# The opening of an encoder block: idle products first, block norms and V's weights in another order, gate forms summed on VectorE

## The chip, the cores and the metric

The kernel runs on one core of a Trainium2 chip. A core has a matrix engine (PE in the profile, with its weight loads as PEld), VectorE (DVE), ScalarE (ACT), GpSimd (POOL) and SyncE (SP), which issues the DMA transfers here. Each engine works through its own instructions in the order in which the program issued them, and waits where an instruction needs something that is not there yet. The metric is the device time of one execution in microseconds (us); the times below are medians of several executions.

## The reference, cut to what matters

The kernel computes one layer of an encoder on 1024 tokens of 1024 channels, in float32:

```python
u = rms_norm(x, norm1_g)
q, k, v, cb, cc, ch, ga, gb = split(u @ w_in)      # 512 x 6, then 1024 x 2 columns
q, k = rms_norm per head (8 heads of 64)
y_a = neighbourhood_attention(q, k, v, rpb) @ w_attn_branch
y_b = (cb * conv3(cc * ch)) @ w_conv_branch
x = x + (sigmoid(ga) * y_a + sigmoid(gb) * y_b) @ w_o
x = x + relu(rms_norm(x) @ w_mlp_in)**2 @ w_mlp_out
```

The change lies in the first step, `u`, in the product for `v`, and in the preparation of `ga` and `gb`.

## The kernel before, in words

**Numbers in two halves.** Every float32 matrix is scaled by powers of two and written as two float16 matrices, a high part and a residual: ScalarE rounds (line 290 for weights, 420 for activations, 482 for forms), and a second engine subtracts the rounded value from the scaled one (lines 278 or 276, 422, 484). One product is three passes of matmuls: high by high, high by residual, residual by high. A unit of 24 matmuls does one block of 128 tokens with one group of columns over 1024 channels.

**Block norms.** x comes in eight blocks of 128 tokens. For each, the generator `norm` (line 414) squares on ScalarE with a row sum (417), then runs a chain of small VectorE operations with a square root on ScalarE in it (390 to 399), then the high part on ScalarE (420) and the residual on VectorE (422): eight steps, and `ln_step(b, n)` issues the next n of block b. Blocks 0 to 2 are transposed on PE (`ln_trans`, 424: eight transposes for each half, copied out by ScalarE and VectorE), blocks 3 to 7 by a DMA that SyncE issues (`ln_turn`, 436).

**Weights.** A `Chunk` is a group of columns: V in two chunks of 256 columns (two loads of 512 KB each), Q and K of 512 (four loads each). `prep` finds the scale (row sums on VectorE or ScalarE; a product with a tile of ones, line 179, adds over partitions; a few integer operations make a power of two of it; line 253 makes it a scale for every row) and splits the weights, load by load. Loads share five buffers, so that each later load is issued on SyncE when an earlier one has been split (line 281). For V, the second load of each chunk is scaled and subtracted on GpSimd (276, 287); all else is subtracted on VectorE (278). `tick(n)` issues the next n steps of such preparations.

**Units.** `v_unit(b, j, steps, ticks)` multiplies block b by chunk j of V (by both chunks where j is None: blocks 3 to 7), counts one more in `units`, issues the copy of the unit before it out of PSUM (508, 509), and then lets `step` and `tick` issue other work. `apart(mark, n)` makes a generator stand still until `units` has reached mark + n, so it fixes where in the order an instruction is issued, not when it runs. Q's eight units and K's eight follow, with per-head norms of what they give (`qk_vec`, 574: out of PSUM by ScalarE at 577, squared at 578, reduced at 581), and K's weights are squared while Q's units run (line 241) and split in the last of them.

**Forms for the gates.** `sforms` (467) makes four sums or differences of half rows of block n and block n + 4 for each n of 0 to 3, for a product of the gates with seven instead of eight sub-products much later: ScalarE scales the rows of the two blocks (474), GpSimd does the four sums (480), ScalarE rounds (482), VectorE subtracts (484), and `sform_store` (487) stores 1 MB to DRAM through SyncE, one unit later. The float32 sums have one buffer, the rounded forms two: the third form waits until the first has been stored. `SFORM` (465) holds the unit count at which each begins. The rows of x that it reads lie where Q's result goes later, so all four must be stored before the fourth unit of Q has ended (`formed`).

**Order around the change.** Lines 514 to 561 write it out by hand: V's first chunk and blocks 0 and 1, then V's second chunk with blocks 2 and 3, then eleven rounds p with one V unit each (from p = 1) and the steps of blocks 3 to 7, one block in two rounds at first. Q's weights are pushed at p = 3; their ones product is issued after p = 7 and their splitting follows in rounds 9 and 10.

Of the kernel before, what the change touches and what calls it, by code (L numbers as in the profile page):

```python
# [52 lines left out]
def encoder_block(ctx: ExitStack, tc: tile.TileContext, x, weights, cols, gqk, rel, masks, out):  # L53
# [79 lines left out]
    def tick(n=1):  # L133

        for _ in range(n):
            i = 0
            while i < len(bg):
                r = advance(bg[i])
                if not r:
                    bg.pop(i)  # L140
                elif r == WAIT and side[0]:
                    i += 1
                else:
                    break
# [5 lines left out]
    def flush():  # L150
        forced[0] = True
        while bg:
            tick()
            step()
        forced[0] = False
# [4 lines left out]
    def apart(mark, n=3, of=units):  # L160
        while of[0] < mark + n and not forced[0]:
            yield WAIT
# [7 lines left out]
        forced[0] = False  # L170
    ones, turn = base.tile([128, 132], BF16, name="ones"), [0]
    V.memset(ones, 1.0)

    def ones_col():
        turn[0] = (turn[0] + 1) % 4
# [24 lines left out]
    def settle():  # L200
        while late:
            late.pop(0)()
# [17 lines left out]
    class Chunk:  # L220


        def __init__(self, kind, widths, tag, rows, half, more):
            self.kind, self.bank = kind, {"V": "o", "Q": "o", "K": "s", "C": "d"}.get(kind)
            self.tag, self.rows, self.widths, self.more = tag, rows, widths, more
            self.offs = []
            self.raw, self.ready, self.half, self.pool = [], more > 0, half, () if half is None else (1,)
            self.split = False

        def prep(self):  # L230
            n = len(self.widths)
            nk = sum(k for k, _ in self.widths)
            rm, a, b, s = (cols_of("prep", i) for i in (nk, 1, 1, 1))
            self.inv = keep()
            tot = sum(k * w for k, w in self.widths)
            if self.kind in "QKCG":
                self.parts = wsp.tile([128, 2, tot], F16, name="w16_ws", tag="ws")
                for p, (k, w) in enumerate(self.widths):
                    while len(self.raw) <= p:
                        yield WAIT  # L240
                    A.activation(self.parts[:, 1, :k * w].bitcast(BF16), self.raw[p][:, :k * w], AF.Square,
                                 accum_out=sc[:, at(rm, p)])
                    yield
                V.tensor_reduce(sc[:, a], sc[:, at(rm, 0, n)], axis=AX, op=OP.add)
                c = ones_col()
                V.tensor_tensor(c, sc[:, a], sc[:, gm2], op=OP.mult)
                yield from apart(units[0], 2 if self.kind == "Q" else 3)
                yield from all_sum(c, b, bank(self.bank) if self.bank else anybank(), 1e-36)
                yield from pow2_half(b, 14, s, self.inv, more=self.more)
            else:  # L250
                yield from self.largest(rm, a, b)
                yield from pow2(b, 14, s, self.inv, False, more=self.more)
            V.tensor_scalar(sc[:, rm], sc[:, self.rows], sc[:, s], None, op0=OP.mult)
            yield
            while done[0] < self.first or self.tag not in wpool:
                yield WAIT
            if self.half is not None:
                if not self.half:
                    vhome.append(wsp.tile([128, 2, 2, tot], F16, name="w16_v", tag="ws"))
                self.parts = vhome[0][:, self.half]  # L260
            elif self.kind not in "QKCG":
                self.parts = wpool[self.tag].tile([128, 2, tot], F16, name="w16_" + self.tag, tag=self.tag)
            f = o = 0
            todo = []
            for p, (k, w) in enumerate(self.widths):
                todo.append((p, [(i * w, w, rm.start + o + i) for i in range(k)], f))
                f += k * w
                o += k
            prev, scaled = None, {}
            for it in todo + [None]:  # L270
                if prev:
                    p, parts, f = prev
                    for o, m, c in parts:
                        hi, lo = (self.parts[:, w, f + o:f + o + m] for w in range(2))
                        if p in self.pool:
                            G.tensor_tensor(lo, scaled[p][:, o:o + m], hi, op=OP.subtract)
                        else:
                            V.scalar_tensor_tensor(lo, self.raw[p][:, o:o + m], sc[:, c:c + 1], hi,
                                                   op0=OP.mult, op1=OP.subtract)
                    done[0] += 1  # L280
                    load_upto(done[0] + 5)
                if it:
                    p, parts, f = it
                    if p in self.pool:
                        scaled[p] = w1p.tile([128, 1024], F32, name="scaled", bufs=1)
                        for o, m, c in parts:
                            G.tensor_scalar(scaled[p][:, o:o + m], self.raw[p][:, o:o + m], sc[:, c:c + 1], 1.0,
                                            op0=OP.mult, op1=OP.mult)
                    for o, m, c in parts:
                        A.activation(self.parts[:, 0, f + o:f + o + m], self.raw[p][:, o:o + m], AF.Copy,  # L290
                                     scale=sc[:, c:c + 1])
                prev = it
                self.split = it is None
                yield
# [129 lines left out]
    def ln_trans(u16, b, dst):  # L424
        for s in range(2):
            pt = bank16("o")
            for k in range(8):
                T.transpose(pt[:, k * 128:(k + 1) * 128], u16[:, s, k * 128:(k + 1) * 128], ident)
            o = dst[:, s, :, b * 128:(b + 1) * 128]
            i = pt.rearrange("p (k t) -> p k t", k=8)  # L430
            if s == 0:
                A.activation(o, i, AF.Copy)
            else:
                V.tensor_copy(o, i)
# [27 lines left out]
    GS = dram.tile([128, 4, 4, 2, 512], F16, name="gs")  # L462

    turned, formed = [0], [0]
    SFORM = (6, 8, 10, 12)

    def sforms():

        for n, start in enumerate(SFORM):
            yield from apart(start, 0)  # L470
            assert turned[0] >= n + 5
            z = []
            for b in (n, n + 4):
                A.activation(xt[:, b], xt[:, b], AF.Copy, scale=sc[:, at(ys, b)])
                z += [xt[:, b, :512], xt[:, b, 512:]]
            f = wqk.tile([128, 4, 512], F32, name="sform", bufs=1)
            v = wqk.tile([128, 4, 2, 512], F16, name="s16", bufs=2)
            for o, a, b, op in ((2, z[0], z[2], OP.subtract), (0, z[2], z[3], OP.subtract),
                                (1, f[:, 0], z[0], OP.subtract), (3, z[1], f[:, 1], OP.add)):
                G.tensor_tensor(f[:, o], a, b, op=op)  # L480
            yield from apart(start, 2)
            A.activation(v[:, :, 0], f, AF.Copy)
            yield
            V.tensor_tensor(v[:, :, 1], f, v[:, :, 0], op=OP.subtract)
            fg.append(sform_store(n, v))
# [6 lines left out]
    def ln_step(b, n=1):  # L492
        for _ in range(n):
            advance(ln[b])
# [17 lines left out]
                               for k in range(8) for sa, sw in PASSES]), post, steps, ticks)  # L512

    push(cV[0])
    ln_step(0, 2)
    tick()
    ln_step(0, 5)
    ln_step(1)
    tick(3)
    ln_step(0)  # L520
    ln_step(1)
    tick(4)
    ln_trans(u16[:, 0], 0, UT)
    flush()
    ln_step(1, 5)
    ln_step(1)
    ln_step(2, 2)
    push(cV[1])
# [1 line left out]
    v_unit(0, 0, 0, 0)  # L530
    ln_step(2, 4)
    ln_trans(u16[:, 1], 1, UT)
    ln_step(2, 1)
    tick(3)
    ln_step(2)
    tick(4)
    ln_step(3, 2)
    ln_trans(u16[:, 2], 2, UT)
    ln_step(3, 4)
    fg.append(qk_gain())  # L540
    fg.append(sforms())
    V.tensor_reduce(sc[:, gm2], sc[:, g1], axis=AX, op=OP.max, apply_absolute_value=True)
    mul(gm2, gm2, gm2)
    for p in range(11):
        if p == 3:
            flush()
            push(cQ)
        if 0 < p < 6:
            v_unit(p % 3, p // 3, 1, 2)
        elif p:  # L550
            v_unit(p - 3, None, 2, 4)
        for q in (p,) if p < 6 else (2 * p - 6, 2 * p - 5):
            c = q // 2 + 3
            if c < 8 and q % 2 == 0:
                ln_step(c, 2)
                ln_turn(u16[:, c % 4], c, UT)
                turned[0] = c + 1
            if c < 7:
                ln_step(c + 1, 3)
    settle()  # L560
    flush()

# [1105 lines left out]
```

## Time and profile before

| | us |
|---|---|
| median of 3 runs | 1248.99 (1246.95 to 1254.03) |
| the profiled execution | 1247.16 |
| its span, first to last instruction | 1245.3 |
| PE busy in it | 1201.1 |
| VectorE, ScalarE, GpSimd busy | 925.3, 764.9, 440.4 |
| PE busy in 0 to 80 us | 60.2 |
| PE busy in 80 to 160 us | 80.0 |

A row of the profile's timeline gives start, duration, engine, line, operation, the tile written and the tiles read, shape, and a count where several are merged; in brackets stands how long the engine stood idle before and what ended that. A row of the groups gives busy time and mean duration in ns after the bar. A row of the windows gives busy time of PE, PEld, DVE, ACT and POOL in a stretch, each with its number of instructions, then the granted clock of PE (1.00 is full), the share of time in which the DMA engines worked, and GB/s. Engine names with a q (SPq, PEq) are the queues that issue.

### The profile page before, as it was taken

The numbers are of one execution on the slowest core, as the hardware profiler recorded it, in microseconds if no ns is written. First come the engines' busy times: TensorE is split into PE (matmuls) and PEld (weight loads), VectorE is DVE, ScalarE is ACT, GpSimd is POOL, SyncE is SP. The second block draws the span as 40 slices with busy tenths as digits, with TensorE's granted clock in tenths as the row PEclk, the third lists the DMA queues.
The fourth block names the chain that finished last, engine by engine and source line by source line (L and its number), as shares of the span: only waits on it lengthen the run. The fifth ranks groups of instructions, "written<-read, shape, count | busy, mean of one in ns | idle before, by whom it ended". The sixth has DMA issues, their size and how long they took to land. (4 is left out here: it accounts for less than half of the span.)

```text
span 1245.3 us, 17058 instructions
## 1 busy us (share of the span) xinstructions
PE 1201.1 (96%) x6294; PEld 576.3 (46%) x6294; DVE 925.3 (74%) x1733; ACT 764.9 (61%) x1177; POOL 440.4 (35%) x297
## 2 busy tenths in 40 slices
PE   5989998998999999999997999999999999999998
PEld 3534444554444444444456544444444444444444
DVE  6668778988557686887677645554546999998997
ACT  6777567777464454545657877877855763645430
POOL 2440002231231111101002756556557463463562
PEclk8999999999999999999998999999999999999999
DMA  6558455657552211215376444543574744435202
GB/s 256 108 188 181 82 118 136 138 97 141 123 112 78 68 55 48 68 47 224 95 146 132 152 159 154 186 149 132 185 268 179 275 189 140 176 119 226 102 34 102
DMA packets 170803, 173.35 MB, mean 139 GB/s; under 512 B 131424, under 2 KB 131936, under 8 KB 166624
## 3 DMA queue, kind: packets, MB, share of 16 engines
q1 hardware_dynamic: 170720, 172.27, 47.2%
q8 instruction: 49, 0.80, 0.3%
q14 instruction: 34, 0.28, 0.1%
HBM read 102.51 MB, written 37.75 MB: 113 GB/s over the span
## 5 line engine op out<-in xcount | busy, mean ns | idle before, releaser
L188 PEld LDWEIGHTS <-ops 128*128 128x128 f16 x1356 | 132.5, 98 | 159.3 <-issue 2.4
L188 PEld LDWEIGHTS <-w 128*128 128x128 f16 x1344 | 130.4, 98 | 142.4 <-issue 3.4
L858 PE MATMUL ps_d<-uT,w_ws 128*128 128x512 f16 x528 | 125.4, 379 | 0.0
L188 PE MATMUL ps_d<-ops 128*128 128x512 f16 (+1 forms) x528 | 118.3, 374 | 0.0
L188 PE MATMUL ps_s<-ops 128*128 128x512 f16 x492 | 113.2, 379 | 1.5 <-DVE sc L112 0.8
L1492 ACT ACTIVATE ops<-hf,sc 128x2048 f16<-128x2048 f32 x26 | 52.0, 1998 | 95.8 <-PE ps_o L188 36.3
L1153 POOL TENSOR_TENSOR as<-as 128x512 f32<-128x512 f32 x64 | 87.9, 1374 | 40.7 <-ACT as L1362 37.0
L962 POOL TENSOR_TENSOR tsum<-raw 128x512 f32<-128x512 f32 x28 | 47.2, 1703 | 147.3 <-ACT raw L948 147.3
L188 PEld LDWEIGHTS <-uT 128*128 128x128 f16 x648 | 65.0, 101 | 70.3 <-issue 6.5
L188 PEld LDWEIGHTS <-w_s 128*128 128x128 f16 x588 | 56.8, 98 | 69.4 <-DVE w_s L973 1.9
L188 PE MATMUL ps_d<-u2x,w 128*128 128x512 f16 (+1 forms) x360 | 80.0, 372 | 0.0
L188 PE MATMUL ps_o<-ops 128*128 128x512 f16 x336 | 77.1, 379 | 0.0
L1494 DVE SCALAR_TENSOR_TENSOR ops<-hf,sc,ops 128x2048 f16<-128x2048 f32 x26 | 71.8, 2763 | 5.5 <-ACT ops L1492 5.5
L858 PEld LDWEIGHTS <-w_ws 128*128 128x128 f16 x528 | 50.9, 98 | 52.5
L948 ACT ACTIVATE raw<-raw,sc 128x256 f32<-128x256 f32 x176 | 72.6, 493 | 1.5 <-DMA raw<-in_weights 1.5
L188 PE MATMUL ps_o<-u2T,w 128*128 128x512 f16 (+1 forms) x312 | 70.3, 375 | 0.0
L962 POOL TENSOR_TENSOR gsum<-raw 128x512 f32<-128x512 f32 x14 | 18.7, 1352 | 131.2 <-issue 57.1
L977 ACT ACTIVATE w<-raw,sc 128x512 f16<-128x512 f32 (+1 forms) x28 | 24.6, 927 | 52.9 <-DVE sc L410 52.9
L1386 DVE TENSOR_TENSOR as<-ps_d,as 128x512 f32<-128x512 f32 (+1 forms) x15 | 10.1, 674 | 62.7 <-ACT as L1403 62.7
L188 PEld LDWEIGHTS <-mH 128*128 128x128 f16 x400 | 39.2, 98 | 32.8 <-issue 1.1
L805 ACT ACTIVATE sz<-sz,sc 128x384 f32<-128x384 f32 (+1 forms) x64 | 37.3, 583 | 26.8 <-DVE sc L796 15.8
L188 PE MATMUL ps_s<-u2T,w 128*128 128x512 f16 (+1 forms) x252 | 52.7, 359 | 0.0
(322 smaller groups left out, 2626.7 us busy)
## 6 DMA issues: line engine op xcount, KB each, us to landing
raw<-in_weights SPq DMA_DIRECT2D x90, 512.0 KB, 5.8
hs<-as SPq DMA_DIRECT2D x16, 1792.0 KB, 8.7
hf<-hs SPq DMA_DIRECT2D x26, 1024.0 KB, 7.1
w2x<-in_weights SPq DMA_DIRECT2D x16, 512.0 KB, 8.2
raw<-in_weights SPq DMA_DIRECT2D x16, 384.0 KB, 4.2
xt<-in_x SPq DMA_DIRECT2D x8, 512.0 KB, 10.1
gs<-s SPq DMA_DIRECT2D x4, 1024.0 KB, 6.9
x<-in_x SPq DMA_DIRECT2D x8, 512.0 KB, 9.8
```

The costliest lines, as they stand in the source:

```text
L188: T.matmul(ps, l, r, start=a, stop=b)
L805: A.activation(z, z, AF.Exp, scale=-1.0, bias=sc[:, d["mx"]], accum_out=sc[:, d["sm"]])
L858: T.matmul(ps, l, r, start=a, stop=b)
L948: A.activation(v, v, AF.Copy, scale=sc[:, at(g, 4 * i + k)])
L962: G.tensor_tensor(t[:, o], a, b, op=OP.add)
L977: A.activation(o(0), w, AF.Copy, scale=sc[:, s])
L1153: sub.tensor_tensor(z[o], z[a], z[b], op=op)
L1386: V.tensor_tensor(z[5], ps[6], z[4], op=OP.add)
L1492: A.activation(P[:, 1, 0], hf, AF.Copy, scale=sc[:, Rs])
L1494: V.scalar_tensor_tensor(P[:, 1, 1], hf, sc[:, Rs], P[:, 1, 0], op0=OP.mult, op1=OP.subtract)
```

## The change

- Right after the ones tile is set, PE does 64 products of it with itself, 128 columns each, into a bank that nothing reads.
- All residuals of V's weights are made on VectorE; GpSimd no longer has part in them.
- Block 0's norm runs through to its high part before V's first reduction is issued. Four steps of block 1's norm are issued before V's first chunk is split.
- V unit (1, 0) moves from round 1 to the place right after the transposes of block 1, ahead of the second half of V's second scale. The transposes of block 2 go ahead of the last four steps of that scale. The splitting of V's second chunk begins between the steps of block 3's norm and ends in round 1, which now has no unit.
- The four sums of each form run on VectorE. The forms begin at unit counts 8, 9, 11 and 13 instead of 6, 8, 10 and 12, and are rounded one unit after their start instead of two.
- In rounds 6 to 10 the two steps stand at the end of the round, behind the norms, and there are eight ticks in a round from 7 on instead of four. Q's weights are thus split in rounds 8 and 9.

```diff
     V.memset(ones, 1.0)
+    warming = bank("s")
+    for _ in range(64):
+        T.matmul(warming[:, 0:128], ones[:, 0:128], ones[:, 0:128], start=True, stop=True)
...
-                        if p in self.pool:
-                            G.tensor_tensor(lo, scaled[p][:, o:o + m], hi, op=OP.subtract)
-                        else:
-                            V.scalar_tensor_tensor(lo, self.raw[p][:, o:o + m], sc[:, c:c + 1], hi,
-                                                   op0=OP.mult, op1=OP.subtract)
+                        V.scalar_tensor_tensor(lo, self.raw[p][:, o:o + m], sc[:, c:c + 1], hi,
+                                               op0=OP.mult, op1=OP.subtract)
...
-                    if p in self.pool:
-                        scaled[p] = w1p.tile([128, 1024], F32, name="scaled", bufs=1)
-                        for o, m, c in parts:
-                            G.tensor_scalar(scaled[p][:, o:o + m], self.raw[p][:, o:o + m], sc[:, c:c + 1], 1.0,
-                                            op0=OP.mult, op1=OP.mult)
...
-    SFORM = (6, 8, 10, 12)
+    SFORM = (8, 9, 11, 13)
...
-                G.tensor_tensor(f[:, o], a, b, op=op)
-            yield from apart(start, 2)
+                V.tensor_tensor(f[:, o], a, b, op=op)
+            yield from apart(start, 1)
...
     push(cV[0])
-    ln_step(0, 2)
+    ln_step(0, 7)
     tick()
-    ln_step(0, 5)
     ln_step(1)
     tick(3)
     ln_step(0)
     ln_step(1)
     tick(4)
     ln_trans(u16[:, 0], 0, UT)
+    ln_step(1, 4)
     flush()
-    ln_step(1, 5)
+    ln_step(1)
     ln_step(1)
     ln_step(2, 2)
     push(cV[1])
...
     v_unit(0, 0, 0, 0)
     ln_step(2, 4)
     ln_trans(u16[:, 1], 1, UT)
+    v_unit(1, 0, 0, 0)
     ln_step(2, 1)
+    ln_step(2)
     tick(3)
-    ln_step(2)
+    ln_trans(u16[:, 2], 2, UT)
     tick(4)
     ln_step(3, 2)
-    ln_trans(u16[:, 2], 2, UT)
+    tick(1)
     ln_step(3, 4)
+    tick(1)
...
-        if 0 < p < 6:
+        if p == 1:
+            step()
+            tick(2)
+        elif p and p < 6:
             v_unit(p % 3, p // 3, 1, 2)
-        elif p:
-            v_unit(p - 3, None, 2, 4)
+        elif p > 5:
+            v_unit(p - 3, None, 0, 4 if p < 7 else 8)
...
             if c < 7:
                 ln_step(c + 1, 3)
+        if p > 5:
+            step(2)
```

More of the change, by code (lines that the diff above doesn't have):

```diff
@@ L226, in __init__ @@
             self.offs = []
-            self.raw, self.ready, self.half, self.pool = [], more > 0, half, () if half is None else (1,)
+            self.raw, self.ready, self.half = [], more > 0, half
             self.split = False
@@ L268, in prep @@
                 o += k
-            prev, scaled = None, {}
+            prev = None
             for it in todo + [None]:
```

## The prediction

> **What bounds the kernel now.** I read the page's busy line first, then the waits of PE, then PE's rows in order of time, then the other engines and the SyncE queue between 0 and 125 us, the only stretch whose program the change touches.
>
> ```profile
> PE 1201.1 (96%) x6294; PEld 576.3 (46%) x6294; DVE 925.3 (74%) x1733; ACT 764.9 (61%) x1177; POOL 440.4 (35%) x297
> PE ps_o L179 <- DVE ones L311: 13.4, 2, 9.9
> PE ps_s L188 <- DMA uT<-u: 2.4, 1, 2.4
> PE ps_d L188 <- DVE w_ws L278: 1.4, 2, 0.9
> 13.42 4.90 PE L188 MATMUL ps_d<-w_v,uT 128*128 128x256 f16 x23 [0.34 <-DVE w_v L278]
> 23.87 0.19 PE L179 MATMUL ps_o<-ones 128*128 128x1 bf16 x1 [3.54 <-DVE ones L311]
> 36.03 2.78 PE L188 MATMUL ps_s<-w_v,uT 128*128 128x256 f16 x24
> 64.53 7.04 PE L188 MATMUL ps_s<-w_v,uT 128*128 128x512 f16 x24 [2.35 <-DMA uT<-u]
> 78.40 5.34 PE L188 MATMUL ps_o<-w_ws,uT 128*128 128x512 f16 x24
> 114.68 5.34 PE L188 MATMUL ps_d<-w_ws,uT 128*128 128x512 f16 x24
> 60.00:70.00 10.00, 7.65 (x29) 3.00 (x27) 5.28 (x12) 5.55 (x6) 5.43 (x5) 0.83 0.53 157
> ```
>
> PE is the bound almost everywhere, so what counts is how much earlier or later it gets through the opening. Its holes are the start, 3.54 us for V1's ones product, 2.35 us for block 7's transpose, and 1.4 us for Q's weights. The clock adds to them: 256-column products take 0.213 us each at 13.42 and 0.116 at 36.03; the V unit behind the 2.35 us hole takes 7.04 us where others take 5.34 (1.7 lost; granted 0.83 in that window). From 78.40 PE runs unbroken through K's first unit (114.68 to 120.02). Whether that stays so is decided on VectorE and ScalarE, which work strictly in program order.
>
> **Part 1, idle products.** 64 products of 128 columns at half rate are 64 x 0.107 = 6.8 us from about 1.05 (the ones tile is set by then), so they end between 5.6 (clock soon up) and 7.9. PE's next work is still the ones product at 9.88 and the first V products after 12.7, because block 0's scale does not come sooner:
>
> ```profile
> 7.41 0.16 DVE L102 TENSOR_TENSOR sc<-sc 128x1 f32<-128x1 f32 x1
> 7.61 0.16 DVE L399 SCALAR_TENSOR_TENSOR sc<-sc 128x1 f32<-128x1 f32 x1
> 8.02 1.22 DVE L301 TENSOR_REDUCE sc<-raw 128x4 f32<-128x1024 f32 x1 [0.25 <-DMA raw<-in_weights]
> 9.88 0.16 PE L179 MATMUL ps_o<-ones 128*128 128x1 bf16 x1 [9.88 <-DVE ones L311]
> ```
>
> Block 0's small operations (0.19 us apart) now run before the first reduction, but the second reduction waits for its weights until 8.02 as before. From the end of the idle products to the first V products PE is nearly idle for 5 us or more. At 64.53 a 2.35 us hole was enough to lose the clock. I value the warming at 0; the bound is the 1.2 us by which the first unit (13.42 to 18.32) could end sooner before VectorE's residuals limit it, and nothing below zero, since PE has no other work then.
>
> The Trainium skill ("TensorE: Matmul & The Clock Gate", Part 1) says that the clock rises after about 3.4 us of sustained work and falls after an idle window of that length; its own example of 64 products of 128 columns warms at number 38. By that rule too the clock is up at the end of the idle products and down again before they are of use, and the trace's 0.83 agrees; the sum would be the same.
>
> **Part 2, V0 and V1 residuals on VectorE, new order to 36 us.**
>
> ```profile
> 25.58 0.22 DVE L253 TENSOR_SCALAR sc<-sc 128x8 f32<-128x8 f32 x1
> 30.98 3.29 ACT L290 ACTIVATE w_v<-raw,sc 128x256 f16<-128x256 f32 x8
> 31.58 1.67 DVE L278 SCALAR_TENSOR_TENSOR w_v<-raw,sc,w_v 128x256 f16<-128x256 f32 x4
> 33.22 2.55 POOL L276 TENSOR_TENSOR w_v<-scaled,w_v 128x256 f16<-128x256 f32 x4 [5.41 <-ACT w_v L290]
> 34.56 1.15 ACT L420 ACTIVATE u<-xt,sc 128x1024 f16<-128x1024 f32 x1
> 35.74 1.28 DVE L422 SCALAR_TENSOR_TENSOR u<-xt,sc,u 128x1024 f16<-128x1024 f32 x1 [0.63 <-ACT u L420]
> ```
>
> Four residuals cost 1.67 us on VectorE, 2.55 on GpSimd. For V0 this, with block 1's small operations put ahead, brings block 1's norm 1.3 us forward. V unit (1,0) fills the 3.54 us hole, but the ones product of V1 now stands behind it on PE, and the copy of block 2's transpose stands before V1's scale on VectorE: scale at about 27.3 (25.8 now). ScalarE's high parts come at 27.6 to 30.9 instead of 30.98 to 34.27, and the first four residuals at 28.4 to 30.1. The other four, however, are issued after block 3's residual, which waits for ScalarE (30.9 and 1.15 more), and after block 4's first small operations, which wait for its square (33.1) and root (33.6): 34.1 to 35.8. GpSimd ended at 35.77. So unit (0,1) ends where it did, and what was won before is lost here: 0. If the clock is low for units (0,0) and (1,0) all this is up to 2.4 us later. Block 4's norm, behind the four residuals, starts at 36.4 (34.56 now).
>
> **Part 3, sforms later, their sums on VectorE.**
>
> ```profile
> 57.36 1.13 ACT L420 ACTIVATE u<-xt,sc 128x1024 f16<-128x1024 f32 x1
> L1153 DVE TENSOR_TENSOR form<-form 128x512 f32<-128x512 f32 x16 | 11.0, 690 | 3.7 <-ACT form L1199 2.5 <-ACT form L1176 0.9
> L484 DVE TENSOR_TENSOR s<-sform,s 128x2048 f16<-128x2048 f32 x4 | 9.1, 2287 | 7.7 <-ACT s L482 7.7
> 55.28 2.17 ACT L474 ACTIVATE xt<-xt,sc 128x1024 f32<-128x1024 f32 x2
> 72.43 5.49 DVE L278 SCALAR_TENSOR_TENSOR w_ws<-raw,sc,w_ws 128x512 f16<-128x512 f32 x6
> 112.60 1.40 DVE L278 SCALAR_TENSOR_TENSOR w_ws<-raw,sc,w_ws 128x512 f16<-128x512 f32 x2
> ```
>
> No form stands before the norms any more, so block 7's norm comes at 52.0 instead of 57.36 and its transpose about 5.5 us sooner: the 2.35 us hole and its 1.7 us of clock go, and PE could start Q at 67.3 instead of about 71.4. But the price of the four sums is 4 x 0.69 = 2.76 us per form on VectorE (no such sum ran there at this place; bounds 0.57, from 2048 elements in 2.287, and the row's 0.69, which has the shape and which I take). VectorE in order: sums of form 0 55.2 to 58.0, V4's residual 0.7, Q's scale 1.2, Q's first two residuals 60.7 to 62.1 (two cost 1.40 without GpSimd beside them); then form 0's residual, which waits for ScalarE's high part (1.91 us, row 87.39 below) behind Q's: 64.4 to 66.7; sums of form 1 to 69.5; V5's residual to 70.2; and only then Q's other six residuals, 4.2 us: to 74.4. They end at 77.92 now. Q's first unit thus ends at about 75.0 (78.57 now), 76.5 if its own hole of about 2.3 us lowers the clock: a gain of 2 to 3.5.
>
> **Part 4, what is late next.** Form 1's residual and sums of forms 2 and 3 have moved behind Q's weights.
>
> ```profile
> 62.14 1.04 SPq L489 DMA_DIRECT2D gs<-s  x1
> 71.93 6.34 SPq L210 DMA_DIRECT2D raw<-in_weights  x4
> gs<-s SPq DMA_DIRECT2D x1, 1024.0 KB, 4.7
> gs<-s SPq DMA_DIRECT2D x1, 1024.0 KB, 9.0
> 76.56 1.04 ACT L241 ACTIVATE w_ws<-raw 128x1024 bf16<-128x1024 f32 x1
> 87.39 1.91 ACT L482 ACTIVATE s<-sform 128x2048 f16<-128x2048 f32 x1 [1.00 <-DMA gs<-s]
> 89.21 0.67 ACT L577 ACTIVATE qs<-ps_o,sc 128x512 f32<-128x512 f32 x1
> 94.09 0.67 ACT L577 ACTIVATE qs<-ps_d,sc 128x512 f32<-128x512 f32 x1
> 110.33 0.67 ACT L577 ACTIVATE qs<-ps_d,sc 128x512 f32<-128x512 f32 x1
> 111.57 2.54 ACT L290 ACTIVATE w_ws<-raw,sc 128x512 f16<-128x512 f32 x4
> 117.47 1.40 DVE L278 SCALAR_TENSOR_TENSOR w_ws<-raw,sc,w_ws 128x512 f16<-128x512 f32 x2
> ```
>
> The store of form 0 stands on SyncE's queue behind the four weight loads that wait for Q's residuals, so it goes out at 74.8, not 62.14, and lands 4.7 to 9.0 us later; beside those loads and the next store I take 8: 82.8. Form 2 needs its buffer. So ScalarE's high part of form 2 runs 82.8 to 84.7 and holds up everything behind it: three squares of K (1.04 and some 0.1 for the read-out of each sum) to 88.1, the rows of form 3 (2.17) to 90.3. VectorE's sums of form 3 then end at 93.1, Q block 0's reduction and K's row sum at 94.2, its root 94.4; form 3's high part ends at 96.3, and only then is Q's second unit taken out of PSUM: 96.3 against 89.21, 7.1 late. From there the chain of Q's norms sets its own pace: 89.21 to 110.33 for five units, 4.2 each, against 5.18 from one PE unit to the next (seven from 78.40 to 114.68). Now it just catches up with PE before K's weights are split (111.57, residuals to 118.87, K's unit ends 120.02). Late by 7.1 it does not: K's residuals end at 126.0 and the unit at 126.4. PE stands about 6 us ahead of it, so the clock is low for its start: 0.6 more (0 to 1.7). The cover that goes is the 1 us per unit by which that chain caught up. Later work hangs on PE's order and shifts as a whole.
>
> **Sum.** The opening gives 0; block 7's 4.1 and the 2 to 3.5 by which Q's first unit ends sooner only lengthen PE's wait before K, so what counts is the end of K's first unit: 126.4 - 120.0 = +6.4, clock +0.6: +7.0. The profiled execution took 1247.16 us (span 1245.3), so 1254.2; its median of 1248.99 lies 1.83 higher: 1256.0. Bounds of the terms: store landing in 4.7 us, -2.7; sums at 0.57 each, -1.9; no low clock, -0.6; low clock in the opening, +2.4; store 9.0, +1.0; K's unit fully slowed, +1.1. The likeliest case alone spans 1250.8 to 1260.5.
>
> **Rivals.** (a) *The holes close and nothing follows.* Block 7 gives 2.35 + 1.7, Q 1.8 (7.0 us from 71.4 to 78.4 for its first unit, against 5.18), the opening 0 to 5 if unit (1,0) in the old hole stays won: -5.8 to -11, 1238 to 1243; centre 1241. For it: VectorE is busy 3.32 of 10 us at 80 to 90. Against: that idle time waits for ScalarE, and order, not load, delays Q.
>
> ```profile
> 80.00:90.00 10.00, 10.00 (x48) 4.52 (x47) 3.32 (x8) 7.11 (x12) 5.03 (x4) 1.00 0.68 263
> 110.00:120.00 10.00, 10.00 (x48) 4.54 (x47) 9.55 (x19) 9.72 (x17) 0.91 (x1) 1.00 0.65 141
> ```
>
> (b) *The lag shrinks on the way.* The store lands in 4.7 us and the sums take 0.57 each (-4.6), or K's split is done in the slack that PE's wait gives: K's unit ends 0 to 4 us late, 1249 to 1253; centre 1251. The 9.55 and 9.72 at 110 to 120 speak against much slack. (c) *The warming does not hold*: it is in my sum; if it did hold, unit (0,0) ends 1.2 sooner, and unit (0,1) still waits for 35.8. It moves the case by 1 us only, 1255. (d) *Low clock in the opening* pushes the whole chain back: +2.4, 1258; inside my own range.
>
> **Chances.** The forecast with (c) and (d) 0.50, (b) 0.32, (a) 0.18. About 0.5% (6.2 us) is what a measurement of this kernel tells from no change. Slower by more takes most of the forecast's case, 0.47; faster by more most of (a), 0.16; within, the rest, 0.37. Range: leaving the fast half of (a) and the slow tail out, 1242 to 1261.
>
> **What would show it.** Right: the idle products end by 8 us and the rows after 12.7 are at half rate; V1's last residuals end near 35.8; no DMA wait before V's last unit; Q's first unit waits for VectorE and ends near 75; the form 2 high part waits for a store; a hole of about 6 us on PE before K's first unit, waiting for L278 or L290. Wrong: PE unbroken at 110 to 125, K's first unit ending before 118, or Q starting at 67 without a wait.

## The result and the profile after

| us | before | changed |
|---|---|---|
| median, 8 runs of each side by side | 1248.55 (1246.95 to 1254.03) | 1256.43 (1255.71 to 1257.67) |
| the profiled execution (its span) | 1247.16 (1245.3) | 1257.05 (1255.2) |
| PE busy, 80 to 160 us | 80.00 | 72.58 |
| ratio of the times | | 1.0065, 95% interval 1.0054 to 1.0076 |

The changed kernel is slower by 0.65% in the ratio, by 7.9 us in the medians. The forecast was 1256.0 with the case "slower by more than 0.5%" as the likeliest. The line numbers have moved by the added lines: 191 is now the unit's matmul, 285 and 278 the splitting of weights, 415 the high part of a norm, 475 the sums of a form, 477 its high part, 484 its store, 580 the read-out of Q and K.

The windows view of the changed kernel (busy time of PE, PEld, VectorE, ScalarE and GpSimd, each with its number of instructions, then the granted clock, the DMA share and GB/s) shows the stretch in which the time goes, the row of before first:

```profile
80.00:160.00 80.00, 80.00 (x374) 36.29 (x373) 59.54 (x168) 50.19 (x90) 6.85 (x6) 1.00 0.66 151
80.00:160.00 80.00, 72.58 (x326) 32.11 (x324) 57.63 (x157) 49.73 (x83) 1.82 (x2) 0.94 0.58 144
```

PE is idle there for 7.4 us, and its clock is 0.94; before it was neither. The timeline of the changed kernel, rows of PE (start, duration, what was done; in brackets the idle time before it and what ended that), answers to the rows shown of before at 13.42, 36.03, 64.53, 78.40 and 114.68:

```profile
1.06 6.13 PE L175 MATMUL ps_s<-ones 128*128 128x128 bf16 x64 [1.06 <-DVE sc L349]
...
13.78 5.07 PE L191 MATMUL ps_d<-w_v,uT 128*128 128x256 f16 x23 [0.99 <-DVE w_v L278]
...
36.33 1.57 PE L191 MATMUL ps_d<-w_v,uT 128*128 128x256 f16 x11 [1.35 <-DVE w_v L278]
37.74 2.78 PE L191 MATMUL ps_s<-w_v,uT 128*128 128x256 f16 x24
...
63.72 5.34 PE L191 MATMUL ps_s<-w_v,uT 128*128 128x512 f16 x24
...
72.25 3.91 PE L191 MATMUL ps_d<-w_ws,uT 128*128 128x512 f16 x17 [1.67 <-DVE w_ws L278]
75.99 5.34 PE L191 MATMUL ps_o<-w_ws,uT 128*128 128x512 f16 x24
...
119.52 0.59 PE L191 MATMUL ps_d<-w_ws,uT 128*128 128x512 f16 x1 [6.67 <-ACT w_ws L285]
120.58 7.57 PE L191 MATMUL ps_d<-w_ws,uT 128*128 128x512 f16 x23 [0.47 <-DVE w_ws L278]
127.99 5.34 PE L191 MATMUL ps_o<-w_ws,uT 128*128 128x512 f16 x24
```

The idle products end at 7.19 and the first V products behind them run at half rate all the same (5.07 us for 23, at a granted clock of 0.50). V's last unit at 63.72 has no wait for a transpose any more and no low clock. Q's second unit starts 2.4 us sooner than before (75.99 against 78.40). Then comes one hole of 6.67 us ahead of K's first unit, and that unit itself is slow: 7.57 us for 23 products. K's second unit starts at 127.99; before it started with the end of the first, 114.68 + 5.18 = 119.86. So K is 8.1 us late.

The same timeline, rows of VectorE, ScalarE and SyncE's queue, tells why:

```profile
28.57 0.15 DVE L185 TENSOR_SCALAR sc<-ps_o 128x1 f32<-128x1 f32 x1
35.80 1.67 DVE L278 SCALAR_TENSOR_TENSOR w_v<-raw,sc,w_v 128x256 f16<-128x256 f32 x4
53.68 1.15 ACT L415 ACTIVATE u<-xt,sc 128x1024 f16<-128x1024 f32 x1 [0.33 <-DVE sc L394]
71.45 4.06 DVE L278 SCALAR_TENSOR_TENSOR w_ws<-raw,sc,w_ws 128x512 f16<-128x512 f32 x6
75.92 2.16 SPq L484 DMA_DIRECT2D gs<-s  x2
80.27 0.69 DVE L475 TENSOR_TENSOR sform<-xt,sform 128x512 f32<-128x512 f32 x1
83.37 1.91 ACT L477 ACTIVATE s<-sform 128x2048 f16<-128x2048 f32 x1 [7.45 <-DMA gs<-s]
96.43 0.67 ACT L580 ACTIVATE qs<-ps_o,sc 128x512 f32<-128x512 f32 x1
118.77 2.54 ACT L285 ACTIVATE w_ws<-raw,sc 128x512 f16<-128x512 f32 x4
124.66 1.40 DVE L278 SCALAR_TENSOR_TENSOR w_ws<-raw,sc,w_ws 128x512 f16<-128x512 f32 x2
```

ScalarE stands still for 7.45 us until form 0's store, issued at 75.92 behind the weight loads, has landed, and then rounds form 2. Most of these 7.45 us it would have stood still in any case: VectorE's sums of form 2 end at 80.96, so the store alone costs the last 2.4. Q's second unit leaves PSUM at 96.43 (89.21 before), the splitting of K's weights begins at 118.77 (111.57 before) and ends at 126.06.

### The profile page after: what moved, and what is told of

It is laid out like the page before. It is cut to its first block, busy times and chain, and to the rows that moved or that the text cites. A ratio compares the mean times of both kernels' runs of the same rounds, so it can differ in the third digit from the quotient of the medians.

```text
span 1255.2 us, 17169 instructions
## 1 busy us (share of the span) xinstructions
PE 1212.4 (97%) x6358; PEld 583.7 (47%) x6358; DVE 934.2 (74%) x1757; ACT 765.0 (61%) x1177; POOL 408.4 (33%) x265
## 5 line engine op out<-in xcount | busy, mean ns | idle before, releaser
L1389 DVE TENSOR_TENSOR as<-ps_d,as 128x512 f32<-128x512 f32 (+1 forms) x15 | 10.1, 674 | 62.7 <-ACT as L1406 62.7
L191 PE MATMUL ps_d<-w_ws,uT 128*128 128x512 f16 x192 | 45.8, 395 | 8.8 <-ACT w_ws L285 6.7
```

The source lines that it names most:

```text
L191: T.matmul(ps, l, r, start=a, stop=b)
```

## The experiments

Each kernel was timed beside the kernel before on the same chip. The first four take the change apart.

**Without the idle products.** The changed kernel less the three added lines.

```diff
-    warming = bank("s")
-    for _ in range(64):
-        T.matmul(warming[:, 0:128], ones[:, 0:128], ones[:, 0:128], start=True, stop=True)
```

> The changed kernel without its 64 idle products. My theory (the loss comes from the order on VectorE and ScalarE before K's first unit; the warming lapses before it is of use): nothing changes, 1255.4 to 1257.4 us, and the first V unit's 23 products take about 4.9 to 5.1 us as they do with the idle products (5.07). Rival (the warming helps the opening): 1 to 3 us slower, 1257.5 to 1259.5. Rival (the idle products cost): faster by 1 us or more.

Measured: 1255.87 us (1252.74 to 1260.38), ratio to before 1.0066 (1.0045 to 1.0086); not to be told from the changed kernel. The timeline of this kernel, rows of PE:

```profile
13.81 3.95 PE L188 MATMUL ps_d<-w_v,uT 128*128 128x256 f16 x23 [0.99 <-DVE w_v L275]
...
36.01 2.78 PE L188 MATMUL ps_s<-w_v,uT 128*128 128x256 f16 x24
...
119.04 0.58 PE L188 MATMUL ps_d<-w_ws,uT 128*128 128x512 f16 x1 [7.16 <-ACT w_ws L282]
```

The first V unit isn't slower without them (3.95 against 5.07 us in these two executions), and the hole before K is as long. The idle products are worth nothing that these runs can tell.

**The new opening alone.** The changed kernel with forms and rounds as before.

```diff
-    SFORM = (8, 9, 11, 13)
+    SFORM = (6, 8, 10, 12)
...
-                V.tensor_tensor(f[:, o], a, b, op=op)
-            yield from apart(start, 1)
+                G.tensor_tensor(f[:, o], a, b, op=op)
+            yield from apart(start, 2)
...
-            v_unit(p - 3, None, 0, 4 if p < 7 else 8)
+            v_unit(p - 3, None, 2, 4)
...
-        if p > 5:
-            step(2)
```

> The opening of the changed kernel (idle products, V residuals on VectorE, new order up to round 5) with the forms and the rounds 6 to 10 of the kernel before. My theory: V1's last residuals end at 37.5 instead of 35.8, and all norms behind them run 1.7 us late; the loss before K's first unit is not there. 1249 to 1251 us, K's first unit ends at 120 to 122. Rival (the opening is what costs): 1254 to 1257.

Measured: 1250.13 us (1248.73 to 1254.82), ratio 1.0015 (1.0002 to 1.0027). **The new rounds and forms alone**, the same edit the other way round, made to the kernel before:

> The opening of the kernel before, with the forms and rounds 6 to 10 of the changed kernel. My theory: the loss stays, less the 1.7 us by which the new opening ends later: 1253.5 to 1256 us; Q's second unit leaves PSUM at 94 to 96 (89.2 before, 96.4 in the changed kernel), and PE waits 4 us or more before K's first unit. Rival (the opening is what costs): 1245 to 1249.

Measured: 1253.02 us (1250.70 to 1260.95), ratio 1.0043 (1.0026 to 1.0059). The rows of PE, first of the opening alone, then of the rounds alone:

```profile
68.01 8.27 PE L191 MATMUL ps_s<-w_v,uT 128*128 128x512 f16 x24 [3.88 <-DMA uT<-u]
...
118.15 5.34 PE L191 MATMUL ps_d<-w_ws,uT 128*128 128x512 f16 x24
```

```profile
73.15 5.34 PE L188 MATMUL ps_o<-w_ws,uT 128*128 128x512 f16 x24
...
118.48 0.58 PE L188 MATMUL ps_d<-w_ws,uT 128*128 128x512 f16 x1 [7.04 <-ACT w_ws L290]
```

With the new opening alone block 7's transpose comes later than before (a hole of 3.88 us instead of 2.35, and 8.27 instead of 7.04 us for the unit), Q and K are 3.5 us late in this execution (118.15 against 114.68 for K's first unit, more than I expected), and K has no hole. With the new rounds alone Q's second unit starts 5.25 us sooner (73.15 against 78.40), more than in the changed kernel, and the hole before K is there in full. The two parts add up (+1.6 and +4.5 us in the medians, +7.9 together, within some 2 us), and the loss before K belongs to the rounds and forms.

**The sums of the forms on GpSimd again.** The changed kernel with one line back.

```diff
-                V.tensor_tensor(f[:, o], a, b, op=op)
+                G.tensor_tensor(f[:, o], a, b, op=op)
```

> The changed kernel with the four sums of each form on GpSimd again, everything else as changed. My theory (lateness and order, not VectorE's load): the sums take about 5.1 us on GpSimd instead of 2.7 in the same chain, VectorE is freed of them ahead of Q's residuals; the two nearly cancel: 1255.5 to 1259 us, and the wait before K's first unit stays at 5 us or more. Rival (the 11 us of load on VectorE are the loss): 1249 to 1253, the wait before K's first unit under 3 us.

Measured: 1257.10 us (1255.34 to 1258.63), ratio 1.0065 (1.0048 to 1.0082). The rows of ScalarE and PE in this kernel:

```profile
82.24 1.91 ACT L477 ACTIVATE s<-sform 128x2048 f16<-128x2048 f32 x1 [4.80 <-POOL sform L475]
...
119.89 0.58 PE L191 MATMUL ps_d<-w_ws,uT 128*128 128x512 f16 x1 [6.73 <-ACT w_ws L285]
```

Form 2 now waits for GpSimd's sums until nearly the same moment, and the hole before K stays. The engine of the sums is not the cause.

**A home for forms 2 and 3 that need not wait for a store.** They are rounded into a free part of the tile of normalised rows.

```diff
-            v = wqk.tile([128, 4, 2, 512], F16, name="s16", bufs=2)
+            v = (wqk.tile([128, 4, 2, 512], F16, name="s16", bufs=2) if n < 2 else
+                 u16[:, 2 * n - 4:2 * n - 2].rearrange("p b s (h m) -> p (b s) h m", h=2))
```

> The changed kernel with the rounded forms 2 and 3 in the two halves of the tile of the block norms that are free by then, so that form 2 need not wait for the store of form 0. My theory (that wait is one of the terms): form 2's high part starts at 81.0 to 81.7 instead of 83.4, the wait before K's first unit is 4 to 5 us instead of 6.7, and the kernel takes 1253.5 to 1255 us. Rival (something else holds ScalarE there, the store only happens to end then): 1256 to 1257.

Measured: 1252.70 us (1249.60 to 1254.83), ratio 1.0028 (1.0017 to 1.0039). The rows of PE:

```profile
117.67 0.59 PE L191 MATMUL ps_d<-w_ws,uT 128*128 128x512 f16 x1 [4.75 <-ACT w_ws L285]
...
125.48 5.34 PE L191 MATMUL ps_o<-w_ws,uT 128*128 128x512 f16 x24
```

Form 2's high part starts at 81.48 instead of 83.37, as soon as its sums are done, and K's second unit 2.5 us sooner (125.48 against 127.99). In the medians the wait for the store was worth 1256.43 - 1252.70 = 3.7 us; the intervals of the two ratios leave some 2 us either way. About half of the loss is left, and so is a hole of 4.75 us.

**Without the arithmetic of forms 2 and 3.** The changed kernel, but the scaling of their rows, the sums, the rounding and the residuals of these two forms are left out and zeros stored in their place, so the gates are incomplete.

```diff
+            if n > 1:
+                v = wqk.tile([128, 4, 2, 512], F16, name="s16", bufs=2)
+                G.memset(v, 0.0)
+                yield
+                fg.append(sform_store(n, v))
+                continue
```

> The changed kernel without the arithmetic of forms 2 and 3: GpSimd writes zeros into their buffers, and these are stored, so part of the gates' result is left out. My theory (the late forms make the chain of Q's norms late, and that makes K's weights late): the wait before K's first unit goes (under 1 us), Q's first unit keeps its gain of about 2.5 us, 1245.5 to 1248.5 us. Rival (the wait before K comes from the opening or from the order of K's own steps): the wait stays at 3 us or more, 1251 to 1256.

Measured: 1245.42 us (1243.30 to 1248.13), ratio 0.9974 (0.9964 to 0.9983). The rows of PE:

```profile
75.35 5.34 PE L191 MATMUL ps_o<-w_ws,uT 128*128 128x512 f16 x24
...
111.64 5.34 PE L191 MATMUL ps_d<-w_ws,uT 128*128 128x512 f16 x24
116.82 5.34 PE L191 MATMUL ps_o<-w_ws,uT 128*128 128x512 f16 x24
```

PE is unbroken from Q into K, as the theory said. The two forms, put among Q's read-outs, are the cause of the lag: with them 127.99, without them 116.82 for K's second unit.

**K's weights split earlier.** The changed kernel with nine steps of preparation instead of three after Q's sixth unit.

```diff
-        unit(tok_mms(ps, actU, b, ch, 8, 512, 0), post, 4, 3)
+        unit(tok_mms(ps, actU, b, ch, 8, 512, 0), post, 4, 9 if n == 5 else 3)
```

> The changed kernel with nine instead of three ticks in the sixth unit of Q, so that the splitting of K's weights is issued one to two units sooner, ahead of the norms of Q's last blocks; the forms are as late as they were. My theory (the loss is nothing but K's weights standing behind the late norms): the wait before K's first unit is under 1 us, 1245.5 to 1249 us. Rival (the lateness shows in another place, a bank that has not been emptied or K's norms): 1251 to 1256.

Measured: 1252.16 us (1250.35 to 1254.64), ratio 1.0028 (1.0017 to 1.0038): the hole went, but not the time that was expected with it. The rows of PE and VectorE:

```profile
112.83 0.38 PE L191 MATMUL ps_d<-w_ws,uT 128*128 128x512 f16 x1 [0.51 <-ACT w_ws L285]
...
119.88 1.40 DVE L278 SCALAR_TENSOR_TENSOR w_ws<-raw,sc,w_ws 128x512 f16<-128x512 f32 x2
120.66 1.25 PE L191 MATMUL ps_d<-w_ws,uT 128*128 128x512 f16 x5 [1.60 <-DVE w_ws L278]
121.76 5.34 PE L191 MATMUL ps_o<-w_ws,uT 128*128 128x512 f16 x24
```

K's first unit starts 6.7 us sooner, and is then fed piece by piece: it takes 8.9 us instead of 5.2, because the last residuals stand behind the norms of Q and end at 121.3. A single long wait had become several short ones.

**Together.** The opening of before, the rounds of the change, the home without the store's wait, and the nine steps.

> The opening of the kernel before, forms and rounds of the changed kernel, forms 2 and 3 rounded into the free tile, and nine ticks in the sixth unit of Q. My theory: Q's second unit starts at about 73 instead of 78.4, nothing waits before K's first unit, so the 5 us stay: 1241.5 to 1245.5 us. Rival (what is won before Q is lost again in the Q and K stage, which VectorE and ScalarE bound): 1247 to 1252.

Measured: 1246.73 us (1244.53 to 1252.07), ratio 0.9989 (0.9974 to 1.0004), which can't be told from before and misses the 1241.5 to 1245.5 of the theory. The rows of PE:

```profile
72.55 5.34 PE L188 MATMUL ps_o<-w_ws,uT 128*128 128x512 f16 x24
...
116.78 1.25 PE L188 MATMUL ps_d<-w_ws,uT 128*128 128x512 f16 x5 [1.66 <-DVE w_ws L278]
117.87 5.34 PE L188 MATMUL ps_o<-w_ws,uT 128*128 128x512 f16 x24
```

Of the 5.85 us won at Q's second unit (72.55 against 78.40) 2.0 are left at K's second (117.87 against 119.86). Three more kernels change only how many steps of preparation follow a unit of Q or K. **Fourteen after Q's sixth**, so that the whole split stands in one piece:

```diff
-        unit(tok_mms(ps, actU, b, ch, 8, 512, 0), post, 4, 9 if n == 5 else 3)
+        unit(tok_mms(ps, actU, b, ch, 8, 512, 0), post, 4, 14 if n == 5 else 3)
```

> The combination with fourteen preparation steps after Q's sixth unit instead of nine: all eight splits of K's weights stand in one piece ahead of the read-out of Q's sixth unit. Theory (order): the residuals end about 4 x 1.40 us after the first, near 115, ahead of what K's first unit needs, so K's first unit (108.9) still waits a little for its first pieces but ends near 115, K's second unit near 115 (117.87 in the combination), median 1243 to 1245. Rival (no room on VectorE and ScalarE): the read-out of Q's sixth unit comes 1.3 us later and the norms of Q that follow push K's read-outs behind, K's second unit not before 117, median 1246 to 1249.

Measured: 1247.20 us (1245.92 to 1249.03), ratio 0.9986 (0.9976 to 0.9996). **Five after every unit of Q and K** (the last argument is 5):

> The combination (opening of before, rounds and forms of after, forms 2 and 3 without the wait for a store), now with five preparation steps after every unit of Q and K instead of three, nine after Q's sixth. K's square sums and its scale are then issued one unit of Q earlier, and the splitting of K's weights is spread over Q's last two units instead of half of it standing behind the read-out of Q's sixth. Theory (it was the order on VectorE and ScalarE that fed K's first unit piece by piece): PE unbroken from Q's second unit (72.5) through K's first, K's second unit near 114.1 (117.87 in the combination, 119.86 before), median 1242 to 1244. Rival (VectorE and ScalarE have no more room between 75 and 120 us; 9.55 of 10 us busy at 110 to 120 in the combination): the waits stay or move into Q's last units, K's second unit at 117 or later, median 1246 to 1249.

Measured: 1247.10 us (1244.42 to 1251.04), ratio 0.9988 (0.9977 to 1.0000). Both missed the time. On K's second unit the theory was right with fourteen (115.29, expected near 115) and not with five (116.39, expected near 114.1). The kernel before, then the one with fourteen, then the one with five, rows of PE and VectorE:

```profile
168.07 0.69 DVE L597 TENSOR_TENSOR k<-qs,k 128x512 f16<-128x512 f32 x1 [0.70 <-ACT k L595]
172.02 0.48 DVE L796 CUSTOM_DVE_ANT_0 sz<-ps_s,bias,sc 128x256 f32<-128x256 f32 x1 [3.01 <-DMA kD<-k]
```

```profile
115.29 5.34 PE L188 MATMUL ps_o<-w_ws,uT 128*128 128x512 f16 x24
...
160.81 5.34 PE L188 MATMUL ps_o<-uT,w_ws 128*128 128x512 f16 x24 [1.32 <-ACT qs L580]
167.84 0.69 DVE L600 TENSOR_TENSOR k<-qs,k 128x512 f16<-128x512 f32 x1 [0.70 <-ACT k L598]
```

```profile
116.39 5.34 PE L188 MATMUL ps_o<-w_ws,uT 128*128 128x512 f16 x24
...
159.15 5.34 PE L188 MATMUL ps_o<-uT,w_ws 128*128 128x512 f16 x24 [1.13 <-ACT qs L580]
167.90 0.69 DVE L600 TENSOR_TENSOR k<-qs,k 128x512 f16<-128x512 f32 x1 [0.70 <-ACT k L598]
```

K's second unit is 4.6 and 3.5 us ahead of before, but the last residual of a key (k) comes at 167.84 and 167.90 against 168.07. VectorE's first step on the attention's scores waits for the transpose of that key (172.02 in the row of before, 171.79 and 171.85 in the two). The norms of Q and K on ScalarE and VectorE are a second chain, as long as PE's: what PE wins ahead of it, PE gives back at a wait for a bank (1.1 to 1.3 us, "qs") or at the attention.

**Five after every unit of Q, three after K's.**

```diff
-        unit(tok_mms(ps, actU, b, ch, 8, 512, 0), post, 4, 9 if n == 5 else 3)
+        unit(tok_mms(ps, actU, b, ch, 8, 512, 0), post, 4, 5 if n < 8 else 3)
```

> As the combination with five preparation steps after every unit of Q, but three again after every unit of K, so that the convolution's weights do not stand ahead of K's norms on ScalarE and VectorE. Theory (the norms of K, a chain on ScalarE and VectorE, set when the attention starts, and in the kernel with five steps throughout the convolution's splits pushed them back; there K's last key half ended at 168.6, as in the kernel before at 168.8): K's second unit near 116.4 as with five steps, K's last key half at 165.5 to 167, the first attention product that had 2.38 us of idle time ahead of it comes 2 us sooner, median 1244.5 to 1246. Rival (that chain's own length, not its order, sets it): last key half at 167.5 or later, median 1246.5 to 1248.

Measured: 1244.95 us (1244.25 to 1246.70) against 1248.72 of before, ratio 0.9971 (0.9956 to 0.9986). It is the fastest complete kernel here. The rows of PE and VectorE:

```profile
116.25 5.34 PE L188 MATMUL ps_o<-w_ws,uT 128*128 128x512 f16 x24
166.32 0.69 DVE L600 TENSOR_TENSOR k<-qs,k 128x512 f16<-128x512 f32 x1 [0.70 <-ACT k L598]
...
329.55 5.34 PE L188 MATMUL ps_s<-uT,w_ws 128*128 128x512 f16 x24
```

The last key comes 1.6 us sooner than with five throughout, as the theory said. But the trace keeps no more than 0.95 us of all this at the end of the attention (329.55 against 330.50, the row below), and the profiled executions differ by 0.8 us (1246.35 against 1247.16), where the medians differ by 3.8. The gain over before is therefore real by its interval, and its size, and that over the other combinations, whose intervals overlap with it, are open. The row of PE in the kernel before:

```profile
330.50 5.34 PE L188 MATMUL ps_s<-uT,w_ws 128*128 128x512 f16 x24
```

## Why the prediction was right, and where it was not

The time (1256.43 against 1256.0), the sign and the mechanism held. That the time is met to 0.4 us is in part luck, since misses in both directions nearly cancel. Point by point:

- **Part 1, idle products, 0.** Right. They ended at 7.19, the granted clock fell to 0.50 at 9.51 and stayed there to 19.75, the work from 12.4 on ran at half rate, and leaving them out changed nothing that the medians can tell. Rival (c), a warming that holds, is out. The granted clock of 0.83 that I called in agreement came behind a hole of 2.35 us: it shows that a hole can lower the clock, and not how long a hole must be; the last section has what the traces say of that.
- **Part 2, opening, 0, with up to 2.4 lost at a low clock (rival (d)).** The zero fell, the bound held. V1's scale came at 28.57 instead of 27.3 and its last residuals ended at 37.47 instead of 35.8, so the V unit at 37.74 came 1.7 us later than its counterpart at 36.03 before, and block 7's norm at 53.68 instead of 52.0. In the kernel without idle products, whose first unit happened to run faster (3.95 us), that V unit started at 36.01: there the zero holds. So the low clock of the first units is what I had priced and should not have left out of the sum, since the row at 13.42 before already showed it. This rests on single executions; in the medians the opening alone cost 1.6 us.
- **Part 3, holes at block 7 and Q.** Right in the changed kernel: no wait at V's last unit, Q's residuals end at 75.51 (74.4), Q's second unit starts at 75.99 (75.0 to 76.5), 2.4 sooner (2 to 3.5). The rounds alone gained 5.25 there (73.15): the opening takes 2.8 us of what this part can give.
- **Part 4, what is late next.** Right to within a microsecond up to K: form 2's high part at 83.37 (82.8), Q's second read-out at 96.43 (96.3), K's residuals to 126.06 (126.0). The landing took 7.4 us from the issue where I took 8, and the hole of "about 6 us" was 6.67. That the two forms among Q's read-outs cause it is shown by leaving them out. My bound of 2.7 us for a store that lands sooner is about the store's share: 2.4 us by the sums' end at 80.96, 1.9 by the kernel with another home (3.7 in its median, with some 2 us of uncertainty). The rest is the forms' own work in that place.
- **Low clock at K, +0.6.** Mis-sized. 23 products took 7.57 us instead of the 5.1 of full rate, and the unit ended at 128.15 instead of 127.0: K's second unit came 8.1 us late instead of 7.0. Part of that is this execution's: in the other four kernels with such a hole (4.75 to 7.16 us) the same 23 products took 6.19 to 6.91 us.
- **Sum.** The profiled execution was 1257.05 where I had 1254.2. "Shifts as a whole" was too simple: the lag is 8.1 us at K, 6.3 at 330 us and 9.9 at the end. In the attention the changed kernel waits less for a transposed tile (1.12 us at 213.39, where before waits 2.80 at 206.85). Later the low clock makes 2.2 us of the difference. After a hole of 7.02 us that both kernels have near 670 us it stays low for longer in the changed one (0.9 us), and behind the next hole it falls in that one only (1.3 us; rows of before, then of the changed kernel):

```profile
705.47 0.16 PE L179 MATMUL ps_s<-ones 128*128 128x1 bf16 x1 [3.09 <-DVE ones L929]
705.49 2.75 PE L188 MATMUL ps_o<-u2T,w 128*128 128x512 f16 x12
713.34 0.16 PE L182 MATMUL ps_s<-ones 128*128 128x1 bf16 x1 [3.22 <-DVE ones L932]
713.36 4.08 PE L191 MATMUL ps_o<-u2T,w 128*128 128x512 f16 x12
```

By the last section this depends on the execution, so the 9.9 us of the profiled executions say less than the 7.9 of the medians, which are nearer to my 7.0.

- **Rival (a)**, holes close and nothing follows, is what the kernel without the arithmetic of two forms shows, at 1245.4 rather than 1241. The 3.05 us that it wins at Q's second unit (75.35 against 78.40) are all there at K's (116.82 against 119.86) and in the medians (1245.42 against 1248.54); what (a) had too high is the gain, 5.8 to 11 us. **Rival (b)**, a lag of 0 to 4 us at K, is out: it was 8.1.

Four of my later expectations (K's weights split earlier, together, fourteen steps, five steps) missed the time for what looks like one reason. I priced an earlier split of K's weights by the hole on PE, and took it that PE's idle time would then be won. But VectorE and ScalarE had little time left: the same instructions, put earlier, stood behind the norms of Q or ahead of those that came next, and these were waited for in their turn. The rows show these waits; no run takes the norms out to prove it.

## What to carry to other kernels

When work leaves the place where it made a hole, follow it on its engines, in program order, to the next thing queued behind it, and include the queue that a store stands in: here forms that were issued later closed 4 us of holes and opened one of 6.67 us forty microseconds later. Before you price a hole as time to be won, check the second chain beside it: if its engines end at the same time as PE, an earlier start moves the wait and wins a fraction. A buffer that must be stored before it can be used again is a wait on a DMA queue; a free tile elsewhere took away part of this loss (3.7 of 7.9 us in the medians) with one changed statement.

## What the runs showed of the hardware

- **Idle products and the first unit.** The first 23 products of V (256 columns) took 5.07, 5.07, 4.23, 5.07, 5.06 and 5.03 us in the six kernels with the idle products and 4.90, 5.06, 3.95, 4.35, 4.16, 5.13 and 3.98 in the seven without; 24 at full rate take 2.78 (the row at 37.74). So the unit runs at half rate for a part that changes from execution to execution, and the idle products did not shorten it. In the six kernels with idle products the granted clock falls to 0.50 between 8.83 and 12.14 us, ahead of these 23 products each time. Before its first change in a trace the granted clock can't be relied on: in the kernel before it reads 1.00 from 14 to 16 us, where a product takes 0.213 us.
- **When a hole costs the clock.** Behind a hole of 1.67 us Q's first unit went on at full rate (17 products in 3.91 us); behind 2.35 and 3.88 us the units took 7.04 and 8.27 instead of 5.34, and behind 6.67 us 23 products took 7.57. But behind 3.09 us at 705.47 in the kernel before nothing was lost. What decides is where the hole lies. Read in narrow windows, the granted clock of the changed kernel falls at 9.51, 26.58, 115.33, 671.70 and 712.66 us and rises at 19.75, 33.41, 125.57, 678.53 and 716.07: all of these lie whole multiples of 3.413 us apart, and so do the changes in the kernel before (21.37, 28.20, 65.75, 69.16, 663.08, 669.91), from another starting point. The clock thus goes by windows of 3.413 us that begin at another moment in each execution. In the window that ends at 65.75 PE was busy for 1.22 us, and the clock fell; in the one that ends at 712.66, for 0.87 us, and it fell. The 3.09 us hole was cut in two by the end of a window at 704.04 (counted on from 669.91), PE was busy for 1.75 and 1.99 us in the two windows, and the clock stayed. The Trainium skill ("TensorE: Matmul & The Clock Gate", Part 1) says that the clock falls after an idle window of about 3.4 us, and that these windows run freely, whatever the kernel does. The second agrees with these traces. The first doesn't agree as it stands: a window in which PE was busy for 1.22 us was enough.
- **A store behind loads.** A 1 MB store of a form lands 3.8 to 10.1 us after its issue in these kernels. Form 0's held ScalarE until 7.4 us after its issue in the changed kernel, and until 8.9 us after it with the rounds alone (issued at 73.07, high part at 81.97), both times with weight loads issued just before it. No run takes the loads away, so their share is open.
